# Attention's transposes on VectorE and through DRAM, and the first down product in plain products, in a hybrid decoder layer

## The chip, the cores and the metric

The kernel runs on one core of a Trainium2 chip. The metric is the time of one execution in device microseconds (us). Three runs of the kernel before took 1603.06, 1602.11 and 1602.8 us, so its time is the median, 1602.8 us. One further execution was recorded by the hardware profiler. Its span, from the first to the last instruction, is 1600.6 us.

The engines: TensorE (PE in the profile; its weight loads are PEld) multiplies matrices and accumulates in PSUM; VectorE (DVE), ScalarE (ACT) and GpSimd (POOL) work element by element; SyncE (SP) and GpSimd also issue DMAs.

## The reference

One decoder layer is applied to 256 prompt tokens and to 8 samples of 8 new tokens each, all with the same weights and all in fp32.

```
xn = rms_norm(x, g_mix)
b_gate, c_gate, h_conv, q, k, v, gate_c, gate_a = split(xn @ w_in)     # D = 2048
u = c_gate * h_conv
y_conv = (b_gate * causal_dwconv3(u)) @ w_conv_out
attn = window_attend(q, k, v)          # 16 query heads, 4 kv heads, head 64, window 128
#   s = q k^T / 8 + rel_bias[t5_bucket(dist)];  m = max(s, sink)
#   p = exp(s - m) / (sum exp(s - m) + exp(sink - m));  attn = p v
y_attn = attn @ w_attn_out
h = x + (sigmoid(gate_c) * y_conv + sigmoid(gate_a) * y_attn) @ w_o
hn = rms_norm(h, g_ffn)
h = h + (silu(hn @ w_gate) * (hn @ w_up)) @ w_down                     # FF = 5632
y = rms_norm(h, g_fin)
```

The prompt attends within itself in bands of 128 queries; each sample attends to 128 cached keys and its own 8. Outputs are y, the last 128 rows of k and v, and the convolution's state, for both groups.

## The kernel before, in words

All 320 tokens (256 + 64) are the columns of every tile, and features lie on the 128 partitions. Each weight is read once from memory in tiles of 512 KB (`wraw`, 4 buffers, DMAs issued by SP). ScalarE copies a tile to a reduced format (`whi`, L128) and VectorE subtracts that from it (`wlo`, L129; 3 buffers each). The activations are kept as two parts in the same way. A product is three matmuls for each block of 128 features by 128 outputs, high weight by high rows, high weight by low rows, low weight by high rows, each with 320 columns and the sum in PSUM (`product`, L175 is its matmul). The low one is issued three blocks later (`passes`), which gives VectorE time. A weight tile gives 24 such matmuls. The rows stand in memory in an interleaved pattern of 16 by 5 by 4 (`fives`, `turns`, `row_tiles`), and the products' matmuls read them through it.

TensorE's order is the order of the program: kv, then q, then four rounds of C, H and B (the convolution), then eight rounds of gate_conv, gate_attn and the two output projections (`gc`, `ga`, `yc`, `ya`), then `wo`, then the feed-forward layer in two halves of 28 and 16 blocks of 128 features, each with its gate and up products (`fg`, `fu`) and then its down product, then the last norm. Attention has no stage of its own. It is a generator that `product` advances by a step after each weight tile (`tick`), so its instructions stand between the products' tiles on every engine, in the order in which the code yields: eight units of a kv head and two query heads for the prompt (scores, softmax, normalisation, four 128 by 128 transposes `pp` at L586 which TensorE makes from the weights of attention and `ident`, two masked copies `pT`, then `po`, weights by values), then the samples (scores `pss`, transposes `spp` and `spn`, weights by values `spo`). k and v of the tokens are turned into rows by TensorE too (`pk`, L493 and L496). The relative bias is put in place as one matmul with a one-hot table (`pe_`, L441); it is stored in DRAM (`e_scr`) and read back as a shifted band per unit (`bias`, L523).

The norms' sums over partitions are matmuls by ones (`over_partitions`, L200): `prb` for the first norm, `pss2` for the second, each with two parts that lie contiguously in memory. A `nudge` (L196) is one matmul into a scratch bank that nobody reads; there are four: within kv, ahead of the third q product, ahead of the second `fg`, and ahead of the second half's first `fu`.

The first half's down product (`down(0, c0)`, L962, L966, L970, four times 512 outputs) has, for each 128 features, a moving operand of 512 columns for the high weight (`a_move`, 128 of its columns the low part of tokens), a matmul with the high weight as the moving operand (`dl`, L966, 512 columns), and one of 320 columns for the low weight.

## Time and profile before

| | us |
|---|---|
| three runs | 1603.06, 1602.11, 1602.8 |
| median | 1602.8 |
| profiled execution, span | 1600.6 |
| median of the runs less the span | 2.2 |
| TensorE busy in the span | 1592.1 (99%) |
| VectorE | 885.6 (55%) |
| ScalarE | 651.4 (41%) |
| GpSimd | 78.3 (5%) |

The profile's page gives busy time by engine, the span in 40 slices, the DMA queues, the chain of work that ended last, and groups of instructions by line. The timeline gives single instructions: the start of one, its length and its count if equal ones follow each other. Matmuls overlap, so the length of one (0.30 us) is not its price. The price is the distance from one start to the next.

### The profile page before, as it was taken

To read this page: it belongs to the slowest core of one execution; us is meant where nothing else is said; L and a number is where in the kernel's file an instruction comes from. 1 tells how busy PE (TensorE), PEld (TensorE's weight loads), DVE (VectorE), ACT (ScalarE), POOL (GpSimd) and SP (SyncE) were. 2 spreads that over 40 slices of the span, in tenths; PEclk is the share of its full clock that TensorE was granted. 3 is DMA by queue.
4 is the path that set the end of the run, shared out by engine and by line. 5 is a ranking of instruction groups with operands and counts; after the bars stand their busy time and mean duration, and the time that the engine had idled before them with its cause. 6 is when DMAs were issued, how large, how long until landed. Compare 5 with 4: busy or idle time off the path is not lost.

```text
span 1600.6 us, 26409 instructions
## 1 busy us (share of the span) xinstructions
PE 1592.1 (99%) x10957; PEld 1555.5 (97%) x10957; DVE 885.6 (55%) x1316; ACT 651.4 (41%) x928; POOL 78.3 (5%) x123
## 2 busy tenths in 40 slices
PE   9999999999999999999999999999999999999998
PEld 9999999999999999999999999998888999999887
DVE  7879565444455555556555555553444455555556
ACT  7555433433333334444333333333333334344443
POOL 1101311000000003320000000000000000000000
PEclk9999999999999999999999999999999999999999
DMA  7554546545444545544444445455555544545552
GB/s 276 174 170 137 182 145 200 167 158 156 154 157 157 157 157 159 158 158 155 154 157 156 157 157 159 158 158 158 155 154 155 157 156 158 158 158 157 182 175 93
DMA packets 74400, 258.14 MB, mean 161 GB/s; under 512 B 8552, under 2 KB 11928, under 8 KB 74152
## 3 DMA queue, kind: packets, MB, share of 16 engines
q1 hardware_dynamic: 71880, 249.86, 49.4%
q0 software_dynamic: 1968, 5.90, 1.3%
q8 instruction: 86, 1.41, 0.4%
q10 hardware_dynamic: 432, 0.69, 0.1%
q14 instruction: 34, 0.28, 0.1%
HBM read 253.30 MB, written 5.08 MB: 161 GB/s over the span
## 4 chain that ended last, share of the span: by engine, by line
PE 99%; DVE 0%; ACT 0%; DVEq 0%; issue 0%
PE fu L175 18%; PE fg L175 18%; PE dn L962 9%; PE gc L175 7%; PE ga L175 7%; PE wo L175 7%; PE dn L970 6%; PE B L175 3%; PE C L175 3%; PE H L175 3%; PE q L175 3%; PE yc L175 3%; PE ya L175 3%; PE dl L966 2%; PE kv L366 2%; PE dn L1114 1%
## 5 line engine op out<-in xcount | busy, mean ns | idle before, releaser
L129 DVE TENSOR_TENSOR wlo<-wraw,whi 128x1024 fp32r<-128x1024 f32 (+1 forms) x460 | 561.7, 1221 | 588.7 <-ACT whi L128 580.5
L128 ACT ACTIVATE whi<-wraw 128x1024 fp32r<-128x1024 f32 (+1 forms) x460 | 485.0, 1056 | 717.3 <-PE dn L962 144.7
L962 PE MATMUL dn<-a_t,whi 128*128 128x512 f32 x640 | 211.1, 385 | 0.0
L175 PE MATMUL fu<-hh_t,whi 128*128 128x320 f32 x704 | 205.3, 302 | 0.0
L175 PE MATMUL fg<-hl_t,whi 128*128 128x320 f32 x704 | 205.3, 302 | 0.0
L175 PE MATMUL fu<-hl_t,whi 128*128 128x320 f32 x704 | 205.3, 302 | 0.0
L175 PE MATMUL fg<-hh_t,whi 128*128 128x320 f32 x704 | 205.3, 302 | 0.0
L175 PE MATMUL fg<-hh_t,wlo 128*128 128x320 f32 x704 | 159.0, 302 | 0.0
L175 PE MATMUL fu<-hh_t,wlo 128*128 128x320 f32 x704 | 159.0, 302 | 0.0
L970 PE MATMUL dn<-a_t,wlo 128*128 128x320 f32 x640 | 146.8, 302 | 0.0
L962 PEld LDWEIGHTS dn<-a_t,whi 128*128 128x128 f32 x640 | 118.8, 188 | 19.3
L175 PEld LDWEIGHTS fg<-hh_t,whi 128*128 128x128 f32 x704 | 131.9, 187 | 0.0
L175 PEld LDWEIGHTS fu<-hh_t,whi 128*128 128x128 f32 x704 | 131.9, 187 | 0.0
L175 PEld LDWEIGHTS fg<-hl_t,whi 128*128 128x128 f32 x704 | 131.8, 187 | 0.0
L175 PEld LDWEIGHTS fu<-hl_t,whi 128*128 128x128 f32 x704 | 131.8, 187 | 0.0
L970 PEld LDWEIGHTS dn<-a_t,wlo 128*128 128x128 f32 x640 | 111.2, 188 | 9.3
L175 PEld LDWEIGHTS fu<-hh_t,wlo 128*128 128x128 f32 x704 | 116.3, 187 | 0.0
L175 PEld LDWEIGHTS fg<-hh_t,wlo 128*128 128x128 f32 x704 | 116.3, 187 | 0.0
L175 PE MATMUL ga<-xl_t,whi 128*128 128x320 f32 x256 | 74.6, 301 | 0.0
L175 PE MATMUL gc<-xl_t,whi 128*128 128x320 f32 x256 | 74.6, 302 | 0.0
L175 PE MATMUL wo<-m_l,whi 128*128 128x320 f32 x256 | 74.6, 302 | 0.0
L175 PE MATMUL gc<-xh_t,whi 128*128 128x320 f32 x256 | 74.6, 301 | 0.0
(313 smaller groups left out, 2681.4 us busy)
## 6 DMA issues: line engine op xcount, KB each, us to landing
wraw<-in_w_in_dram SPq DMA_DIRECT2D x128, 512.0 KB, 3.8
wraw<-in_w_gate_dram SPq DMA_DIRECT2D x88, 512.0 KB, 3.8
wraw<-in_w_up_dram SPq DMA_DIRECT2D x88, 512.0 KB, 3.7
wraw<-in_w_down_dram SPq DMA_DIRECT2D x88, 512.0 KB, 3.6
wraw<-in_w_o_dram SPq DMA_DIRECT2D x32, 512.0 KB, 3.7
wraw<-in_w_conv_out_dram SPq DMA_DIRECT2D x16, 512.0 KB, 3.6
wraw<-in_w_attn_out_dram SPq DMA_DIRECT2D x16, 512.0 KB, 3.6
wraw<-in_w_kv_dram SPq DMA_DIRECT2D x6, 512.0 KB, 7.4
```

What stands on the lines that cost most here:

```text
L128: last["hi"] = nc.scalar.activation(hi, src, AF.Copy)
L129: last["lo"] = nc.vector.tensor_sub(lo, src, hi.bitcast(F32))
L175: last["mm"] = nc.tensor.matmul(turns(fives(ps[c][:, :T])), w[:, k, c * P:(c + 1) * P], turns(x(kc)), start=(kc == 0 and i == 0), stop=(kc ...
L366: last["mm"] = nc.tensor.matmul(turns(fives(ps[c][:, :T])), w[:, k, c * P:(c + 1) * P], turns(x(kc)), start=(kc == 0 and m == 0), stop=(kc ...
L962: nc.tensor.matmul(turns(placed(ps[c])), parts[k][0][:, cs], turns(a_move(k)), start=k == 0, stop=False)
L966: nc.tensor.matmul(low, a_low(k), parts[k][0], start=k == 0, stop=k == nf - 1 and c0 < E0)
L970: last["mm"] = nc.tensor.matmul(turns(placed(ps[c])[:, :, 0:JT]), parts[k][1][:, cs], turns(a_move(k)[:, :, 0:JT]), start=False, stop=k == ...
L1114: nc.tensor.matmul(turns(placed(ps[c])[:, :, JR:]), held[k][0][:, cs], turns(a_move(k)[:, :, JR:]), start=k == 0, stop=k == nf - 1,)
```

## The change

Every transpose of attention leaves TensorE. VectorE transposes 32 by 32 blocks within SBUF (`nc.vector.transpose`), GpSimd's DMAs write the result to a DRAM scratch, in four pieces, one for each group of 32 partitions, so that the blocks also change places (`turned_rows`), and one more DMA reads it back. This holds for k and v (`kv_turn`, then a ScalarE copy in `kv_natural`), for the eight units of the prompt (`prompt_turn`, read back and masked in SBUF in `prompt_values`, a new step after all eight units) and for the samples (`s_scr`, `n_scr`). The one-hot matmul becomes 17 copies on GpSimd. The sums of the norms (`prb`, `pss2`) read their parts through the products' pattern, from rows of tiles that are free at that time (`two_rows`). The last two prompt units' `po` come in one group.

Two nudges go (ahead of the second `fg` and of the second half's first `fu`), and three of 320 columns come: behind `pss`, behind `spo` and ahead of the first `ga`. The first half's down product becomes plain products: three matmuls of 320 columns per block, from rows in the products' pattern (`a_fives`); the results go to `hT` alone.

```diff
-    def two_parts(src, tags=("ta", "tb")):
-
-        n = src.shape[-1]
-        hi, lo = (wk.tile([P, UL], F32R, tag=t, name=u("part"))[:, :n] for t in tags)
-        nc.scalar.activation(hi, src, AF.Copy)
-        nc.vector.tensor_sub(lo, src, hi.bitcast(F32))
+    def two_rows(src, hi, lo):
+
+        nc.scalar.activation(hi, fives(src), AF.Copy)
+        nc.vector.tensor_sub(lo, fives(src), hi.bitcast(F32))
         return hi, lo
...
         for i, x in enumerate(parts):
-            nc.tensor.matmul(out, ones_r, x, start=i == 0, stop=i == 1)
+            nc.tensor.matmul(turns(fives(out)), ones_r, turns(x), start=i == 0, stop=i == 1)
...
+    def turned_rows(name, flipped, blocks, run):
+
+        scr = dr.tile([blocks * B, 4 * run], F32, name=name)
+        rows = scr.rearrange("(b i) (a x) -> a i b x", i=B, x=run)
+        for a_ in range(4):
+            nc.gpsimd.dma_start(rows[a_], flipped[a_ * B:(a_ + 1) * B].rearrange("p (b x) -> p b x", x=run))
+        return scr
...
-    rel = zz.tile([NBK, NH], F32, name="rel")
+    relT = zz.tile([NH, NBK], F32, name="relT")
...
-        parts = two_parts(xacc)
-        nc.vector.tensor_copy(oh_r, oh)
-        nc.scalar.activation(rel_r[:, 0], rel, AF.Copy)
-        nc.vector.tensor_sub(rel_r[:, 1], rel, rel_r[:, 0].bitcast(F32))
-        yield
-        prb, pe_ = ps_aux("prb"), ps_aux("pe_")
-        for i in range(2):
-            nc.tensor.matmul(pe_[:NH, :WIN], rel_r[:, i], oh_r, start=i == 0, stop=i == 1)
+        parts = two_rows(xacc, at_h(7), at_l(7))
+        at, one_each = [_bucket(c) for c in range(WIN)], NBK // 2
+        nc.gpsimd.tensor_copy(e_sb[:, WIN - 1:WIN - 1 + one_each], relT[:, :one_each])
+        for b in range(one_each, NBK):
+            c, n = WIN - 1 + at.index(b), at.count(b)
+            nc.gpsimd.tensor_copy(e_sb[:, c:c + n], relT[:, b:b + 1].to_broadcast([NH, n]))
+        yield
+        prb = ps_aux("prb")
         over_partitions(prb[:, :T], parts)
...
-        nc.vector.tensor_copy(e_sb[:, WIN - 1:2 * WIN - 1], pe_[:NH, :WIN])
         nc.gpsimd.dma_start(e_scr, e_sb)
...
-    def kv_natural(t):
+    def kv_turn(t):
+
         t0, tn = TOK[t]
-        pk = ps_aux(u("pk"))
-        for j in range(2):
-            nc.tensor.transpose(pk[:tn, j * P:(j + 1) * P], vT[:, j, t0:t0 + tn], ident)
-        if t > 0:
-            for j in range(2):
-                nc.tensor.transpose(pk[:tn, 256 + j * P:256 + (j + 1) * P], kT[:, j, t0:t0 + tn], ident)
-        nc.vector.tensor_copy(vn[t][:tn, :], pk[:tn, 0:DKV])
+        nb, zs = tn // B, (vT, kT)[:1 + (t > 0)]
+        run = len(zs) * 2 * B
+        flipped = pr.tile([P, 512], F32, tag="T", name=u("kvT"), bufs=3)[:, :nb * run]
+        blocks = flipped.rearrange("p (b z c j) -> p z c b j", b=nb, c=2, j=B)
+        for i, z in enumerate(zs):
+            nc.vector.transpose(blocks[:, i], z[:, :, t0:t0 + tn].rearrange("p c (b i) -> p c b i", i=B))
+        rows = pr.tile([P, 512], F32, tag="rows", name=u("rows"), bufs=3)[:tn, :4 * run]
+        nc.gpsimd.dma_start(rows, turned_rows(f"kv_scr{t}", flipped, nb, run))
+        return rows.rearrange("p (a z c j) -> p z a c j", a=4, c=2, j=B)
+
+    def kv_natural(t, rows):
+        t0, tn = TOK[t]
+
+        def natural(out, z):
...
+        natural(vn[t], 0)
         if t > 0:
-            nc.vector.tensor_copy(kn[:tn, :], pk[:tn, 256:512])
...
-    def prompt_pt(s):
-        pt = pr.tile([P, 3, 2 * WIN], F32, tag="pT", name=u("pT"), bufs=4)
-        pp = ps_aux(u("pp"))
-        for n in range(4):
-            nc.tensor.transpose(pp[:, n * WIN:(n + 1) * WIN], s[:, n], ident)
-        nc.scalar.activation(pt[:, 0, :], pp[:, 0:256], AF.Copy)
-        for b in range(2):
-            nc.vector.tensor_mul(
-                pt[:, 1 + b, :].rearrange("p (g q) -> p g q", g=2),
-                pp[:, 256:512].rearrange("p (g q) -> p g q", g=2),
-                sides[:, b:b + 1].to_broadcast([P, 2, WIN]),
-            )
-        return pt
+    def prompt_turn(s):
+        flipped = pr.tile([P, 4, 4, B], F32, tag="T", name=u("T"), bufs=3)
+        nc.vector.transpose(flipped.rearrange("p b n j -> p n b j"), s.rearrange("p n (b i) -> p n b i", i=B))
+        return turned_rows(u("p_scr"), flipped.rearrange("p b n j -> p (b n j)"), 4, 4 * B)
+
+    def by_head(x):
+
+        return x.rearrange("p a g j -> p g a j")
+
+    def prompt_masked(pv, sides, pt):
+
+        late = by_head(pt[:, :, 2:4])
+        side = pv.tile([P, 2, 4, B], F32, name=u("side"))
+        for out, m in ((side, 0), (late, 1)):
+            mask = sides[:, m].rearrange("p (a j) -> p a j", j=B).unsqueeze(1).to_broadcast([P, 2, 4, B])
+            nc.vector.tensor_mul(out, late, mask)
+        return by_head(pt[:, :, 0:2]), side, late
...
                 nc.tensor.matmul(
-                    po[par * 64:(par + 1) * 64, b * 256:(b + 1) * 256],
-                    vn[t][:, kv * HD:(kv + 1) * HD], pts[par][:, kb, :], start=st_, stop=sp_,
+                    po[par * 64:(par + 1) * 64, b * 256:(b + 1) * 256].rearrange("p (g a j) -> p g a j", g=2, j=B),
+                    vn[t][:, kv * HD:(kv + 1) * HD], pts[par][kb], start=st_, stop=sp_,
...
+    def prompt_weights(scrs):
+        bias, sc, sm = {}, {}, {}
         bias[0] = bias_load(*units[0])
-        for i in range(len(units) + 3):
...
                 yield
                 sm[i] = prompt_softmax(*units[i], sc[i])
-            if i >= 3 and (i - 3) % 4 == 3:
-                for n in (i - 5, i - 3):
-                    kv, gp = units[n]
-                    prompt_pv(kv // 2, gp, (pts.pop(n - 1), pts.pop(n)))
-            if 0 <= i - 2 < len(units):
-            if 0 <= i - 1 < len(units):
+            if i >= 1:
                 prompt_norm(sc[i - 1], *sm.pop(i - 1))
-            if i >= len(units):
-                yield
+                scrs.append(prompt_turn(sc.pop(i - 1)))
+
+    def prompt_values(pv, scrs):
+        sides = pv.tile([P, 2, WIN], F32, name="sides")
...
+        pts = []
+        for i in range(len(units) + 5):
+            if i < len(units):
+                pts.append(pv.tile([P, 4, 4, B], F32, name=u("pT")))
+                nc.gpsimd.dma_start(pts[i].rearrange("p a n j -> p (a n j)"), scrs[i])
+            if i >= 5:
+                pts[i - 5] = prompt_masked(pv, sides, pts[i - 5])
+            yield
+        for i in range(0, len(units), 2):
+            kv, gp = units[i]
+            prompt_pv(kv // 2, gp, pts[i:i + 2])
+        yield
...
     def sample_attention(sm):
-        kf = sm.tile([P, NB, 2, W2], F32, name="kf")
+        kf = sm.tile([P, NB, 2, W2], F32, tag="kf", name="kf")
...
+        nudge(xh, xl, T)
...
-        pn = sm.tile([P, NB, TS], F32, name="pnew")
-        nc.vector.tensor_copy(pn, s[:, :, WIN:W2])
-        yield
-        ptw = sm.tile([P, NB * P], F32, name="ptw")
-        for h in range(2):
+        flipped = sm.tile([P, NB * W2], F32, tag="kf", name="sT")
+        nc.vector.transpose(
+            flipped[:, :NB * WIN].rearrange("p (c b j) -> p b c j", c=4, j=B),
+            s[:, :, 0:WIN].rearrange("p b (c i) -> p b c i", i=B),
+        )
+        nc.vector.transpose(flipped[:, NB * WIN:], s[:, :, WIN:W2])
+        ptw = sm.tile([P, NKV, NB, B], F32, name="ptw")
+        nc.gpsimd.dma_start(
+            ptw.rearrange("p a b j -> p (a b j)"), turned_rows("s_scr", flipped[:, :NB * WIN], 4, NB * B)
+        )
         pns = sm.tile([64, P], F32, name="pns")
-        nc.vector.tensor_copy(pns, pp[:64, 0:P])
+        nc.gpsimd.dma_start(pns, turned_rows("n_scr", flipped[:, NB * WIN:], 2, B))
+        yield
+        yield
+        yield
+        yield
...
                     nc.tensor.matmul(
                         pos[j][par * 64:(par + 1) * 64, b * 32:(b + 1) * 32],
-                        cv[:, kv * HD:(kv + 1) * HD], ptw[:, b * P + kv * 32:b * P + (kv + 1) * 32],
+                        cv[:, kv * HD:(kv + 1) * HD], ptw[:, kv, b],
...
+        nudge(xh, xl, T)
...
+        rows = []
         for t in range(3):
-            kv_natural(t)
+            rows.append(kv_turn(t))
             yield
         yield from keys_twice()
+        for t in range(3):
+            kv_natural(t, rows[t])
+            yield
...
     def attention():
-        yield from prompt_attention()
+        scrs = []
+        yield from prompt_weights(scrs)
         pr_p.close()
+        with tc.tile_pool(name="pv", bufs=1, side="right") as pv:
+            yield from prompt_values(pv, scrs)
         with tc.tile_pool(name="sm", bufs=1, side="right") as sm:
...
+            if (mp, nm) == (0, "ga"):
+                nudge(xh, xl, T)
...
+    def a_fives():
+
+        per = FH[0] // 2
+        step = per * JS + 16
+        group = -(-(NS * step - 16) // JS) * JS
+        flat = fp.tile([P, LEAD_F + A_ALL], F32R, tag="at", name=u("a_t"))
+        groups = [rows_in(flat, LEAD_C + g * group, step, lambda k: k % per * JS) for g in range(4)]
+        return [lambda k, i=i: groups[2 * i + k // per](k) for i in range(2)]
...
+    def sets_of(nf):
+        sets = [(k, k + 1) for k in range(0, nf, 2)]
+        sets[-2:] = [sets[-2] + sets[-1]]
+        return sets
+    def down_first(c0):
+
+        nf = FH[0]
         ps = [ps_acc(u("dn")) for _ in range(4)]
+        sets = sets_of(nf)
+        for i, ks in enumerate(sets):
             parts = {}
+            for k in ks[::2]:
+                parts |= down_weights(0, c0, k)
             end = i == len(sets) - 1
-            order = [(k, c) for k in parts for c in range(4)]
+            order = [(k, c) for k in ks for c in range(4)]
+            if end or i == 0:
+                order.sort(key=lambda kc: kc[1])
+            for k, c, m in passes(order, end):
+                w, x = ((0, a_hi), (0, a_lo), (1, a_hi))[m]
+                last["mm"] = nc.tensor.matmul(
+                    turns(fives(ps[c][:, :T])), parts[k][w][:, c * P:(c + 1) * P], turns(x(k)),
+                    start=k == 0 and m == 0, stop=k == nf - 1 and m == 2,
+                )
+        for c in range(4):
+            k = c0 // P + c
+            nc.vector.tensor_add(hT[:, k, :], ps[c][:, :T], hT[:, k, :])
...
-        a_move, a_low, a_first, free = a_rows(half)
+        if half == 0:
+            a_hi, a_lo = a_fives()
+        else:
+            a_move, a_low, a_first, free = a_rows(half)
...
-            if half == 0 and fpair == 1:
-                nudge(hh, hl, P)
...
-                over_partitions(pss[:, :T], two_parts(hacc, ("tc", "td")))
+                over_partitions(pss[:, :T], two_rows(hacc, a_hi(FH[0] - 1), a_lo(FH[0] - 1)))
...
-            if half == 1 and fpair == 0:
-                nudge(hh, hl, P)
...
+                if half == 0:
+                    split_to(a_hi(f), a_lo(f), fives(gs[c]))
+                    continue
...
-                if half == 1:
-                    nc.scalar.activation(a_first(f), gs[c][:, 0:P], AF.Copy)
+                nc.scalar.activation(a_first(f), gs[c][:, 0:P], AF.Copy)
...
         for c0 in range(0, D if half == 0 else E0, 512):
-            down(half, c0)
-            if half == 1:
+            if half == 0:
+                down_first(c0)
+            else:
+                down(c0)
```

How the order of instructions changes is shown at three places.

TensorE in the first H product beside attention: `pp` are the four transposes of one prompt unit, the rows around it the product's own matmuls. Before:

```order
L175 MATMUL H_1318<-xh_t,wlo_1375 128x16x5x4
L175 MATMUL H_1319<-xh_t,wlo_1375 128x16x5x4
L586 MATMUL pp_1414<-ident,s_1172 128x128 x4
L175 MATMUL H_1318<-xh_t,whi_1424 128x16x5x4
L175 MATMUL H_1318<-xl_t,whi_1424 128x16x5x4
```

After:

```order
L176 MATMUL H_1334<-xh_t,wlo_1398 128x16x5x4
L176 MATMUL H_1335<-xh_t,wlo_1398 128x16x5x4
L176 MATMUL H_1334<-xh_t,wlo_1398 128x16x5x4
L176 MATMUL H_1335<-xh_t,wlo_1398 128x16x5x4
L176 MATMUL H_1334<-xh_t,whi_1438 128x16x5x4
L176 MATMUL H_1334<-xl_t,whi_1438 128x16x5x4
```

The transposes are gone and one tile's matmuls follow the other's directly.

VectorE in the same stretch, where `den` is a unit's denominator, `s` its weights, `pT` the masked copy of a former unit's transposes and `wlo` a weight tile's low part. Before:

```order
L129 TENSOR_TENSOR wlo_1555<-wraw_1552,whi_1554 128x1024
L577 TENSOR_TENSOR den_1403<-den_1403,es_1404 128x4
L578 RECIPROCAL den_1403<-den_1403 128x4
L589 TENSOR_TENSOR pT_1413<-pp_1414,sides 128x256 x2
L580 TENSOR_SCALAR s_1358<-s_1358,den_1403 128x128 x4
L129 TENSOR_TENSOR wlo_1607<-wraw_1604,whi_1606 128x1024
```

After:

```order
L130 TENSOR_TENSOR wlo_1567<-wraw_1564,whi_1566 128x1024
L582 TENSOR_TENSOR den_1426<-den_1426,es_1427 128x4
L583 RECIPROCAL den_1426<-den_1426 128x4
L585 TENSOR_SCALAR s_1381<-s_1381,den_1426 128x128 x4
L589 STREAM_TRANSPOSE T_1600<-s_1381 128x4x4x32
L130 TENSOR_TENSOR wlo_1626<-wraw_1623,whi_1625 128x1024
```

The two masked copies have left this place, and one transpose of 128 by 512 stands behind the unit's own normalisation, ahead of the next weight tile's low part.

TensorE in the first half's down product, where `a_t` holds the activations and `dn` the four sums. Before:

```order
L962 MATMUL dn_11267<-a_t_7524,whi_11322 128x16x8x4
L966 MATMUL dl_11271<-whi_11322,a_t_7524 128x512
L962 MATMUL dn_11268<-a_t_7524,whi_11322 128x16x8x4
L962 MATMUL dn_11269<-a_t_7524,whi_11322 128x16x8x4
L962 MATMUL dn_11270<-a_t_7524,whi_11322 128x16x8x4
L970 MATMUL dn_11267<-a_t_7524,wlo_11323 128x10x8x4
```

After:

```order
L1015 MATMUL dn_11259<-a_t_7576,whi_11355 128x16x5x4 x2
L1015 MATMUL dn_11260<-a_t_7576,whi_11355 128x16x5x4 x2
L1015 MATMUL dn_11261<-a_t_7576,whi_11355 128x16x5x4 x2
L1015 MATMUL dn_11262<-a_t_7576,whi_11355 128x16x5x4 x2
L1015 MATMUL dn_11259<-a_t_7576,wlo_11356 128x16x5x4
```

Nine matmuls of 512, 512 and 320 columns per block become twelve of 320, in the pattern (16x5x4) that the other products have.

## Rows read from the trace of the kernel before

**Rows 1.** The page: busy time by engine; TensorE's granted clock in 40 slices.

```profile
PE 1592.1 (99%) x10957; PEld 1555.5 (97%) x10957; DVE 885.6 (55%) x1316; ACT 651.4 (41%) x928; POOL 78.3 (5%) x123
...
PEclk9999999999999999999999999999999999999999
```

**Rows 2.** The page: the chain of work that ended last, by engine.

```profile
PE 99%; DVE 0%; ACT 0%; DVEq 0%; issue 0%
```

**Rows 3.** TensorE's timeline, wo and the next product: start us, us, operation, xcount.

```profile
593.92 0.30 PE L175 MATMUL wo<-m_h,whi 128*128 128x320 f32 x1
...
701.45 0.30 PE L175 MATMUL fg<-hh_t,whi 128*128 128x320 f32 x1
```

**Rows 4.** TensorE's timeline at a prompt unit's transposes.

```profile
110.29 0.60 PE L586 MATMUL pp<-ident,s 128*128 128x128 f32 x4
110.64 0.39 PE L175 MATMUL H<-xh_t,whi 128*128 128x320 f32 x1
110.87 0.30 PE L175 MATMUL H<-xl_t,whi 128*128 128x320 f32 x1
```

**Rows 5.** TensorE's timeline at the samples' transposes.

```profile
210.04 1.04 PE L700 MATMUL spp<-ident,s_s 128*128 128x128 f32 x8
...
210.94 0.39 PE L175 MATMUL H<-xh_t,whi 128*128 128x320 f32 x1
211.17 0.30 PE L175 MATMUL H<-xl_t,whi 128*128 128x320 f32 x1
```

**Rows 6.** TensorE's timeline at the one-hot product and the first norm's sum.

```profile
38.50 0.58 PE L175 MATMUL q<-xh_t,wlo 128*128 128x320 f32 x3
39.01 0.29 PE L441 MATMUL pe__589<-oh_r,rel_r 32*16 32x128 f32 x2
...
39.62 0.30 PE L175 MATMUL q<-xh_t,whi 128*128 128x320 f32 x1
```

**Rows 7.** TensorE's timeline from the second norm's sum over a nudge.

```profile
715.18 0.31 PE L175 MATMUL fu<-hh_t,whi 128*128 128x320 f32 x1
...
728.85 0.23 PE L196 MATMUL nudge<-hh_t,hl_t 128*128 128x128 f32 x1
...
729.11 0.30 PE L175 MATMUL fg<-hl_t,whi 128*128 128x320 f32 x1
...
742.40 0.30 PE L175 MATMUL fu<-hh_t,whi 128*128 128x320 f32 x1
```

**Rows 8.** TensorE's timeline, first down product and the product behind it.

```profile
1078.40 0.38 PE L962 MATMUL dn<-a_t,whi 128*128 128x512 f32 x1
...
1266.96 0.30 PE L175 MATMUL fg<-hh_t,whi 128*128 128x320 f32 x1
...
1280.61 0.23 PE L196 MATMUL nudge<-hh_t,hl_t 128*128 128x128 f32 x1
```

**Rows 9.** Busy time by stretch: us, then PE, PEld, DVE, ACT, POOL, PEclk, DMA share, GB/s.

```profile
88.00:145.00 57.00, 57.00 (x421) 55.70 (x420) 51.82 (x132) 32.57 (x91) 7.93 (x18) 1.00 0.52 162
145.00:185.00 40.00, 40.00 (x293) 38.70 (x292) 26.65 (x58) 17.88 (x36) 13.16 (x24) 1.00 0.54 170
```

**Rows 10.** VectorE's groups, 88 to 180 us: operation xcount | busy, mean ns | idle before.

```profile
L589 DVE TENSOR_TENSOR pT<-pp,sides 128x256 f32<-128x256 f32 x16 | 6.1, 416 | 0.0
...
L562 DVE TENSOR_REDUCE mx<-s 128x4 f32<-128x512 f32 x8 | 5.5, 682 | 0.1
```

**Rows 11.** VectorE's timeline, the first norm's reciprocal.

```profile
41.82 2.15 DVE L234 RECIPROCAL r<-r 128x320 f32<-128x320 f32 x1 [0.54 <-ACT r L233]
```

**Rows 12.** GpSimd's timeline, DMA issues.

```profile
42.49 1.48 POOL L523 DMA_DIRECT2D bias<-e_scr  x2
...
126.18 0.74 POOL L523 DMA_DIRECT2D bias<-e_scr  x1
```

**Rows 13.** DMA issues: transfer, queue, xcount, KB each, us from issue to landing.

```profile
bias<-e_scr POOLq DMA_DIRECT2D x8, 256.0 KB, 4.1
kf<-in_cache_kt_dram POOLq DMA_DIRECT2D x4, 256.0 KB, 5.2
...
e_scr<-e_sb POOLq DMA_DIRECT2D x1, 24.0 KB, 1.8
```

More of the change, by code (lines that the diff above doesn't have):

```diff
@@ L23 @@
 NBK = 32
+B = 32
 FF = 5632
@@ L613, in two_to @@
         nc.vector.tensor_sub(dl, src, dh.bitcast(F32))
-    def prompt_attention():
-        units = [(j * 2 + par, gp) for j in range(2) for gp in range(2) for par in range(2)]
-        bias, sc, sm, pts = {}, {}, {}, {}
+    units = [(j * 2 + par, gp) for j in range(2) for gp in range(2) for par in range(2)]
+    def prompt_weights(scrs):
+        bias, sc, sm = {}, {}, {}
         bias[0] = bias_load(*units[0])
-        for i in range(len(units) + 3):
+        for i in range(len(units) + 1):
             if i < len(units):
@@ L936, in h_parts, with down_weights @@
         return parts_of(hT[:, k, :])
-    def down(half, c0):
-        nf, f0 = FH[half], half * FH[0]
+    def down_weights(half, c0, k0):
+        raw = wp.tile([P, 2, 512], F32, tag="wraw", name=u("wraw"), bufs=4)
+        k = half * FH[0] + k0
+        nc.sync.dma_start(raw, w_d[c0 // 512, :, k:k + 2, :])
+        hi = wp.tile([P, 2, 512], F32R, tag="whi", name=u("whi"), bufs=3)
+        lo = wp.tile([P, 2, 512], F32R, tag="wlo", name=u("wlo"), bufs=3)
+        split_to(hi, lo, raw)
+        return {k0 + j: (hi[:, j, :], lo[:, j, :]) for j in range(2)}
@@ L957, in down @@
+    def down(c0):
+        nf = FH[1]
+        ps = [ps_acc(u("dn")) for _ in range(4)]
+        low = ps_aux(u("dl"))
+        sets = sets_of(nf)
+        for i, ks in enumerate(sets):
+            parts = {}
+            for k in ks[::2]:
+                parts |= down_weights(1, c0, k)
+            end = i == len(sets) - 1
+            order = [(k, c) for k in ks for c in range(4)]
             if end or i == 0:
@@ L966, in down @@
                     nc.tensor.matmul(
-                        low, a_low(k), parts[k][0], start=k == 0, stop=k == nf - 1 and c0 < E0
+                        low, a_low(k), parts[k][0], start=k == 0, stop=k == nf - 1
                     )
@@ L983, in down @@
             mark["out"].append(nc.vector.tensor_add(rest, rest, got[:, :, JT:]))
[L984 to L989 removed]
+        nc.scalar.activation(ylow[:, c0:c0 + 512], low, AF.Copy)
     for half in range(2):
@@ L1153, in hybrid_layer @@
         for m, x in enumerate((xhk, xlk)):
-            last["mm"] = nc.tensor.matmul(rowacc, x, wh, start=False, stop=k == nf - 1 and m == 1)
+            last["mm"] = nc.tensor.matmul(rowacc, x, wh, start=k == m == 0, stop=k == nf - 1 and m == 1)
         if k == 3:
@@ L1213 @@
     from concourse.bass_utils import run_bass_kernel_spmd as _run
-    onehot = _np.zeros((NBK, WIN), _np.float32)
-    for c in range(WIN):
-        onehot[_bucket(c), c] = 1.0
     block = _np.zeros((64, NB), _np.float32)
@@ L1248 @@
     arrays, args, outs = {}, {}, []
-    for name, v in [(n, inputs[n]) for n in _INS] + [("c_onehot", onehot), ("c_block", block)]:
+    for name, v in [(n, inputs[n]) for n in _INS] + [("c_block", block)]:
         v = _np.ascontiguousarray(v)
```

52 lines of the change are left out of this document (12 added, 40 removed).

## The prediction, made before the changed kernel ran

> **What bounds the kernel now.** I read the page first: TensorE is busy for 99% of the span, and its granted clock stands at nine tenths or more in all 40 slices [rows 1], which is its upper level of 2.4 GHz. The chain of work that ended last is TensorE for 99% of it [rows 2]. So the time is the sum of TensorE's instruction stream, and an edit is worth what it adds to or takes from that stream, unless it makes TensorE wait.
>
> Then I read the stream's pace from the timeline, as distances between starts. wo has 8 x 16 x 6 = 768 matmuls from 593.92 to 701.45 [rows 3]: 107.53 / 768 = 0.1400 us each. This is the good pace. There is a second one. Behind the sum `pss2`, fu's 96 matmuls take from 715.18 to 728.85, 0.1424 each; from the first matmul behind the nudge, at 729.11, the 95 up to 742.40 go at 0.1399 again [rows 7]. Behind the first down product the same: 1266.96 to 1280.61 is 0.1422 each, up to another nudge [rows 8]. So an odd matmul can leave the stream in a pace 2.3 ns slower per matmul, which lasts until another disturbance; a nudge ended it both times.
>
> **The change part by part, on TensorE.**
>
> Prompt transposes: four `pp` take from 110.29 to 110.64, and the product's next matmul takes 0.23 up to 110.87 where the pace is 0.14 [rows 4]. One unit costs 0.35 + 0.09 = 0.44 us. Eight units: -3.5.
>
> k and v: ten transposes of the same width, in groups of 2, 4 and 4. By [rows 4], 0.44 for each group of four and half of 0.35 for the pair: -1.1.
>
> Samples: nine transposes from 210.04 to 210.94, and 0.23 instead of 0.14 behind them [rows 5]: 0.90 + 0.09, so -1.0.
>
> One-hot product and first sum: three matmuls that start at 38.50 should end their turn at 38.92; the next product's starts at 39.62 [rows 6]. The detour costs 0.70. What remains is the sum's two matmuls; if they run at the good pace, 0.28: -0.4.
>
> The second sum now reads rows in the products' pattern, which should leave no slow pace behind: 96 x 2.4 ns = -0.23 in fu. Behind the down product likewise 96 x 2.2 ns = -0.21 in fg.
>
> Two nudges go. One costs 729.11 - 728.85 = 0.26 where a matmul costs 0.14, so 0.12 each: -0.24 [rows 7]. Three of 320 columns come, at a matmul's 0.14 each: +0.42. One of `po`'s two groups goes, which I put at one such switch, -0.1.
>
> First down product: 112 block rows of nine matmuls take from 1078.40 to 1266.96, 188.56 us [rows 8]. Columns per block row are 4 x 512 + 512 + 4 x 320 = 3840 before and 12 x 320 = 3840 after. 112 x 12 = 1344 matmuls at 0.1400 give 188.16: -0.4. The reorder loses nothing, because the old form already streamed at its columns. If the new rows ran at the slow pace, 1344 x 2.3 ns = +3.1; they have the products' pattern and lie with the products' offsets, so I take the good one.
>
> Sum: -3.5 - 1.1 - 1.0 - 0.4 - 0.23 - 0.21 - 0.24 + 0.42 - 0.1 - 0.4 = -6.8 us.
>
> **What lies beside TensorE, and what it costs if the cover is gone.**
>
> VectorE gains eight transposes of 128 x 512 at the scores, and loses there sixteen masked copies of 0.416, 6.7 us, which return later out of SBUF [rows 10]. No row of before has this transpose. From below, it can't cost less than nothing. From above, the slowest row is the reciprocal, 2.15 us for 320 elements per partition [rows 11], 3.4 for 512. I take the row of its shape, the reduction of 128 x 512, 0.682 [rows 10]: 8 x 0.68 = 5.5, so VectorE's load there stays what it was, 51.82 of 57 us between 88 and 145 [rows 9]. Its cover is the low parts made ahead: three buffers of 24 matmuls, 3.36 us each, so VectorE may run about 6 us late before TensorE waits. The masks return between 145 and 185, where it is busy for only 26.65 of 40. At 3.4 us per transpose, VectorE would need 51.8 - 6.7 + 27.2 = 72.3 us in those 57, and TensorE would wait for some 72.3 - 57 - 6 = 9 us.
>
> The Trainium skill speaks against this edit: "VectorE: DVE Perf Modes", Rules for kernel authors, leaves a 128 x 128 transpose to TensorE where the result may go to PSUM, and its section on the three transpose paths gives 390 ns for TensorE, and 311 ns for VectorE, for 32 x 32 blocks only. The trace has TensorE at about 0.11 us each within the stream, and no row for VectorE. By the page's figure an estimate for one unit is 4 x 0.311 = 1.24 us, 9.9 in all, which would fill 55 of the 57 us and cost little or nothing.
>
> ScalarE loses the prompt's copies out of PSUM and is busy for 32.57 of 57 us [rows 9], so its part is nothing.
>
> The round trips are cover against queue. By the order of the changed program GpSimd issues 98 DMAs where it had 34. An issue takes 0.74 us, also at 126.18 in the stretch where VectorE is at 91% [rows 9, 12], and transfers land 1.8 to 5.2 us after the issue [rows 13]. A unit's trip is four issues, a landing, one issue and a landing: 4 x 0.74 + 1.8 + 0.74 + 2, about 7.5 us. For the prompt, a unit's rows are read back at least four tiles, 13.4 us, ahead of their mask. For the samples, the transposes, eight issues and two landings in a row come to about 12 us against the four added yields, 13.4 us. The samples' cached keys (`kf`), loaded only after `po`, need four issues and 5.2, about 8.2, against about 13.4. So each is hidden, the samples' one with the least to spare. Behind a waiting DMA on GpSimd's queue stand the bias loads of later units and the convolution's products with rb; those are wanted at the end of B, a product of 96 matmuls or 13.4 us later. TensorE's order puts no product behind the round trips but `po` and `spo`, and a wait there holds up everything.
>
> **Rivals.**
>
> A: the forecast, all hidden. 1600.6 - 6.8 = 1593.8 span. The median of the runs lies 2.2 us above the profiled span, so 1596.0. Own range 1594.5 to 1597.5: the terms of the small groups and that 2.2 are each good to about half a microsecond.
>
> B: VectorE becomes the bound between 88 and 145. For it: 91% busy already. Against it: the masks leave. From a transpose of about 1.5 us (51.8 - 6.7 + 12 = 57.1) its lead begins to be eaten, and at 3.4 the wait is 9 us. 1596 to 1605; middle 1599.
>
> C: a round trip is late. For it: 64 more DMAs in order on one queue, trips whose cover exceeds them by only 1 to 6 us. Against it: no issue in the trace is held up by VectorE. Twice the landing times on the samples' trip and on `kf` would give waits of 3 to 6 us: 1599 to 1602.
>
> D, the other side: the slow pace sticks where a nudge has gone or does not take. From the first ga to the last fu of the second half there are 8544 matmuls of 320 columns with no nudge among them (2208 in the rounds of gates, 768 in wo, 22 pairs of 192 in the halves, 1344 in the first down product); at 2.3 ns each the whole is 19.6 us: 1596.0 + 19.6 = 1615.6. It decides from 6.8 / 0.0023 = 2960 matmuls, that is if the slow pace lasts for over some 415 us. For it: two nudges are removed exactly where the slow pace stood before, and both places now rest on the pattern alone. Against it: what left it behind was a sum over contiguous parts and matmuls of 512 columns, and neither is there any more; each change between products of the pattern keeps 0.140 [rows 3].
>
> E: the change saves nothing because the transposes lay in gaps that TensorE has anyway. Against it: there is no gap in the stream around them, and the product's matmuls start 0.14 apart up to the transposes [rows 4, 6]. The time would be 1602.8.
>
> **How the numbers follow.** A 0.70, B 0.10, C 0.10, D 0.07, E 0.03. This kernel's runs can tell about 0.2%, 3.2 us, from no change, so faster means below 1599.6 and slower above 1606.0. Faster: all of A, over half of B, a quarter of C and a little of D, 0.80. Slower: D and the far end of B, 0.08. The same: the rest, 0.12. The range 1594.0 to 1601.5 holds A, most of C and half of B or more; D is left out above.
>
> **What would show it.** In the profile after: no `pp`, `pk` or `spp` on TensorE, and its busy share still at 99%. A product's distance between starts of 0.140 in the first fu, in the second half's first fg and all through the first down product, which takes 188.2 us. STREAM_TRANSPOSE of 128 x 512 near 0.7 us, and VectorE near 91% while scores run. TensorE's waits ahead of `po` and `spo` at nothing. Wrong would be a distance of 0.142 over many products (D), waits of TensorE for `wlo` between 88 and 145 (B), or for `ptw`, `pns` or `pT` (C).

## The result, and the profile after

The changed kernel takes 1607.5 us (median of six runs, 1607.36 to 1607.69) against 1602.8: a ratio of 1.0031 with an interval of 1.0019 to 1.0042. The forecast was 1596.0, faster. It is slower.

The page after, busy time by engine and the chain that ended last by engine:

```profile
PE 1597.2 (99%) x11241; PEld 1581.5 (98%) x11241; DVE 884.7 (55%) x1258; ACT 646.9 (40%) x894; POOL 118.1 (7%) x204
...
PE 99%; DMA 1%; ACT 0%; DVE 0%; ACTq 0%; DVEq 0%; issue 0%
```

TensorE still ends the chain with 99%, as in [rows 1, 2]. So again only its stream has to be read. TensorE's timeline after, at the places of [rows 3, 7, 8] (start us, us, operation, xcount):

```profile
588.25 0.30 PE L176 MATMUL wo<-m_h,whi 128*128 128x320 f32 x1
...
695.77 0.30 PE L176 MATMUL fg<-hh_t,whi 128*128 128x320 f32 x1
...
709.22 0.45 PE L199 MATMUL pss<-a_t,ones_r 128*128 128x320 f32 x2
709.50 0.30 PE L176 MATMUL fu<-hh_t,whi 128*128 128x320 f32 x1
...
723.15 0.30 PE L176 MATMUL fg<-hh_t,whi 128*128 128x320 f32 x1
...
1078.14 0.45 PE L1015 MATMUL dn<-a_t,whi 128*128 128x320 f32 x2
...
1269.29 0.30 PE L176 MATMUL fg<-hh_t,whi 128*128 128x320 f32 x1
...
1487.74 0.39 PE L1040 MATMUL dn<-a_t,whi 128*128 128x512 f32 x1
```

Three stretches tell it all. Up to wo, the changed kernel is 593.92 - 588.25 = 5.7 us ahead, and wo itself runs at 0.140. Behind `pss2`, 96 matmuls of fu take 709.50 to 723.15, 0.1422 each; the down product's 1344 take 191.15 us, 0.1422 each, where before the whole product took 188.56; and the pace holds up to 1487.74, where the second half's down product begins. From fu to there it is 778.24 us. The kernel before had 767.15, from 715.18 [rows 7] to this row of its timeline:

```profile
1482.33 0.38 PE L962 MATMUL dn<-a_t,whi 128*128 128x512 f32 x1
```

So 11.1 us are lost, and 5.7 - 11.1 = -5.4 is the difference of the spans, 1606.0 against 1600.6. From that down product to the end both take 118.3.

What was to be hidden is hidden. Busy time by stretch after (us, PE, PEld, DVE, ACT, POOL, PEclk, DMA share, GB/s), against [rows 9]:

```profile
88.00:145.00 57.00, 57.00 (x417) 57.00 (x416) 53.12 (x132) 31.30 (x86) 21.33 (x42) 1.00 0.62 187
145.00:185.00 40.00, 40.00 (x288) 40.00 (x287) 32.46 (x58) 16.28 (x25) 15.79 (x31) 1.00 0.73 238
```

and VectorE's groups after, 88 to 180 us:

```profile
L130 DVE TENSOR_TENSOR wlo<-wraw,whi 128x1024 fp32r<-128x1024 f32 x26 | 31.9, 1232 | 3.6 <-ACT whi L129 3.3
...
L589 DVE STREAM_TRANSPOSE T<-s 128x512 f32<-128x512 f32 x8 | 5.7, 708 | 0.1
...
L602 DVE TENSOR_TENSOR side<-pT,sides 128x256 f32<-128x256 f32 x6 | 3.8, 625 | 0.8 <-issue 0.8
```

A transpose of 128 x 512 takes 0.708 us where 0.68 was put. VectorE is 93% busy at the scores, and TensorE fills both stretches.

### The profile page after: what moved, and what is told of

The parts are those of the page before. It is cut to its first block, busy times and chain, and to the rows that moved or that the text cites. A ratio compares the mean times of both kernels' runs of the same rounds, so it can differ in the third digit from the quotient of the medians.

```text
span 1606.0 us, 26991 instructions
## 1 busy us (share of the span) xinstructions
PE 1597.2 (99%) x11241; PEld 1581.5 (98%) x11241; DVE 884.7 (55%) x1258; ACT 646.9 (40%) x894; POOL 118.1 (7%) x204
## 4 chain that ended last, share of the span: by engine, by line
PE 99%; DMA 1%; ACT 0%; DVE 0%; ACTq 0%; DVEq 0%; issue 0%
PE fu L176 19%; PE fg L176 19%; PE dn L1015 12%; PE ga L176 7%; PE wo L176 7%; PE gc L176 7%; PE B L176 3%; PE q L176 3%; PE H L176 3%; PE C L176 3%; PE ya L176 3%; PE yc L176 3%; PE dn L1040 3%; PE dn L1048 2%; PE kv L370 1%; PE dl L1044 1%
## 5 line engine op out<-in xcount | busy, mean ns | idle before, releaser
L1015 PE MATMUL dn<-a_t,whi 128*128 128x320 f32 x896 | 165.0, 303 | 0.0
L1015 PEld LDWEIGHTS dn<-a_t,whi 128*128 128x128 f32 x896 | 139.2, 187 | 0.0
L1015 PE MATMUL dn<-a_t,wlo 128*128 128x320 f32 x448 | 105.4, 304 | 0.0
L1015 PEld LDWEIGHTS dn<-a_t,wlo 128*128 128x128 f32 x448 | 75.2, 187 | 0.0
L176 PE MATMUL ga<-xh_t,whi 128*128 128x320 f32 x256 | 74.6, 301 | 0.0
```

The costliest lines, as they stand in the source:

```text
L176: last["mm"] = nc.tensor.matmul(turns(fives(ps[c][:, :T])), w[:, k, c * P:(c + 1) * P], turns(x(kc)), start=(kc == 0 and i == 0), stop=(kc ...
L1015: last["mm"] = nc.tensor.matmul(turns(fives(ps[c][:, :T])), parts[k][w][:, c * P:(c + 1) * P], turns(x(k)), start=k == 0 and m == 0, stop= ...
```

## The experiments

The question is why `pss2` left the slow pace, though its rows were read in the products' pattern, and whether that is the whole loss. The good pace is 0.140 us per matmul, the slow one 0.142. The theories: **N**, the slow pace lasts until some other matmul ends it, and the removed nudge was what ended it; **O**, the sum leaves it because its weights, `ones_r`, lie at another place than a product's weights. In the program as built `ones_r` starts 160 bytes past a multiple of 256, every weight tile 128 past one, and every product's rows, those of `pss2` among them, 64 past one. The rivals: **P**, the plain down product is slow by itself; **R**, the pattern is what leaves the slow pace; **Q**, rows and weights must both be like a product's.

**One nudge back** (e1_nudge_back).

```diff
+            if half == 0 and fpair == 1:
+                nudge(hh, hl, P)
             psg = product(
```

> The changed kernel with one nudge put back, ahead of the second fg product, where the kernel before had it; nothing else differs. Theory N (the loss is the slow pace that the second norm's sum leaves behind, which nothing ends any more until the second half's down product): the 96 matmuls of the first fu stay at 0.142 us each, all 5376 matmuls behind the nudge run at 0.140, which takes 5376 x 2.2 ns = 11.8 us off the 1607.5, less 0.15 for the nudge: 1595.8 us. Rival P (the slow pace belongs to the new places of the activations in the plain down product, and would come with or without the nudge): the down product's 1344 matmuls stay at 0.142, the nudge helps only the pairs ahead of it: about 1601 us.

1595.59 us; ratio to before 0.9954 (0.9939 to 0.9969). TensorE's timeline:

```profile
709.32 0.30 PE L176 MATMUL fu<-hh_t,whi 128*128 128x320 f32 x1
...
722.97 0.22 PE L195 MATMUL nudge<-hh_t,hl_t 128*128 128x128 f32 x1
...
723.23 0.30 PE L176 MATMUL fg<-hl_t,whi 128*128 128x320 f32 x1
...
736.53 0.30 PE L176 MATMUL fu<-hh_t,whi 128*128 128x320 f32 x1
```

fu still takes 13.65 us for 96 (0.1422); behind the nudge 95 take 13.30 (0.140). One instruction gives back 11.9 us of 1607.5. N holds, and P falls: the plain down product runs at 0.140 if it is entered at 0.140.

**The kernel before without its nudge** (e4_before_no_nudge).

```diff
-            if half == 0 and fpair == 1:
-                nudge(hh, hl, P)
```

> The kernel before with one line less: the nudge ahead of the second fg is gone, all else as it was. Theory N (the slow pace that the second norm's sum leaves lasts until something else than a product's matmul comes, and the nudge was all that ended it): the 26 products of pairs two to fourteen, 2496 matmuls, run at 0.1423 instead of 0.1400, +5.7 us, less the nudge's 0.1; the first down product's matmuls of 512 columns then end it: 1608.3 us. Rival (the slow pace would fade by itself, at a product's end or a load): within 1 us of the kernel before, 1602 to 1604 us.

1608.37 us; ratio 1.0033 (1.0020 to 1.0047). The pace does not fade: the last fu ahead of the down product still takes 13.66 for 96.

```profile
1070.71 0.30 PE L175 MATMUL fu<-hh_t,whi 128*128 128x320 f32 x1
...
1084.37 0.38 PE L962 MATMUL dn<-a_t,whi 128*128 128x512 f32 x1
```

So in the kernel before too, one nudge was worth 5.4 us (the kernel before took 1603.01 in these runs). The old down product takes 188.61 us behind the slow pace, 188.56 before, so the loss ended there; the plain one carries it on.

**The ones moved** (e2_ones_moved), no nudge added.

```diff
-    ones_r = cst.tile([P, P], F32R, name="ones_r")
+    ones_r = cst.tile([P, P + 64], F32R, name="ones_r")[:, 56:56 + P]
```

> The changed kernel without any further nudge; only the ones that serve as weights in the norms' sums lie elsewhere, 128 bytes past a multiple of 256, as all weight tiles do, where they lay 160 bytes past one. Theory O (the sum's matmuls leave the slow pace because their weights start at another place within 256 bytes than the products' weights): the two pss2 matmuls take 0.140 each and the first fu behind them 0.140, no slow pace anywhere in the feed-forward layer: 1595.5 us. Theory N in its plain form (any pair that isn't a product's leaves the slow pace, whatever its operands' places): 1607.5 us, unchanged.

1595.53 us; ratio 0.9955 (0.9938 to 0.9971).

```profile
708.93 0.44 PE L199 MATMUL pss<-a_t,ones_r 128*128 128x320 f32 x2
709.21 0.30 PE L176 MATMUL fu<-hh_t,whi 128*128 128x320 f32 x1
...
722.65 0.30 PE L176 MATMUL fg<-hh_t,whi 128*128 128x320 f32 x1
...
1072.09 0.44 PE L1015 MATMUL dn<-a_t,whi 128*128 128x320 f32 x2
...
1260.24 0.30 PE L176 MATMUL fg<-hh_t,whi 128*128 128x320 f32 x1
```

The sum's pair takes 0.28, fu 13.44 (0.140), the down product 188.15. At this place O holds: with the weights 224 bytes further on, the sum takes what two more matmuls of a product would take, and the pace behind it stays. Every later tile moves by 256 bytes with it, but that is not the cause: the probes below have the same shift with the ones at 160, and there `pss2` leaves fu at 0.142.

**The sum from contiguous parts** (e3_sum_contiguous), and **with the ones moved as well** (e5_contiguous_ones_moved).

```diff
-                over_partitions(pss[:, :T], two_rows(hacc, a_hi(FH[0] - 1), a_lo(FH[0] - 1)))
+                over_contiguous(pss[:, :T], two_parts(hacc, ("tc", "td")))
```

> The changed kernel, with the second norm's sum alone read from contiguous parts again, as before; no nudge behind it. Theory R (reading the parts through the products' pattern is what leaves the slow pace): the pace behind it would be 0.140 and the time 1595.6 us. Theories N and O (the sum leaves it in either form, as it did in the kernel before, where fu behind the contiguous sum ran at 0.1424): unchanged within 0.5 us, 1607.5 us.

> The changed kernel without a further nudge, the second sum read from contiguous parts (as in the kernel before) and the ones moved to 128 bytes past a multiple of 256. Theory O alone (only the weights' place decides): fu behind the sum runs at 0.140, 1595.6 us. Rival Q (the pair must be like a product's matmul in both operands, rows in the pattern and weights at 128, to leave the pace alone): the contiguous pair takes over 0.14 each, the slow pace stands behind it, 1607.5 us.

e3 takes 1607.72 us, ratio 1.0031 (1.0019 to 1.0042); e5 1607.48, ratio 1.0028 (1.0017 to 1.0038). e5's timeline:

```profile
708.96 0.45 PE L211 MATMUL pss<-part,ones_r 128*128 128x320 f32 x2
709.25 0.31 PE L176 MATMUL fu<-hh_t,whi 128*128 128x320 f32 x1
...
722.92 0.30 PE L176 MATMUL fg<-hh_t,whi 128*128 128x320 f32 x1
```

fu takes 13.67. R falls, and O alone falls too. At this place Q holds: the changed reading of the rows was needed, and so was the ones' place. As a rule for any pair it is not shown. In the probes below, five contiguous pairs, with ones at 64, 128 or 160, all left 0.140. Those read rows that start 64 bytes past a multiple of 256, as a product's do; in e5 the second of the two parts starts at 96, and no run separates that from the pattern.

**Probes** (p1_probes, p2_probes_320): extra groups ahead of fg, in p1 with nudges of 128 columns ahead of fu, in p2 of 320.

```diff
+    def odd(phase, n=2, flat=False, cols=T):
+        w = ones_w[:, (phase - 160) % 256 // 4:][:, :P]
...
+            if (half, fpair) in probes:
+                odd(*probes[half, fpair])
+            elif (half, fpair) != (0, 0):
+                nudge(hh, hl, T)
```

> The changed kernel with extra matmuls into a bank that nobody reads, each ahead of an fg product, and a nudge ahead of each fu, so that each extra group starts from the good pace and its effect is read from the 96 matmuls behind it. The extra groups: pairs that read rows through the products' pattern with ones as weights at 0, 32, 64, 96, 128, 160, 192 and 224 bytes past a multiple of 256; one matmul of 160 and one of 128; three and four of 160; pairs and single ones from contiguous columns. Theory O: the pairs at 128 leave 0.140, most others, 160 among them, leave 0.142. Theory N in its plain form: every pair leaves 0.142 behind, whatever its place. A third reading (the pace is a phase which each extra matmul shifts by a bit, so that the count decides): one, two, three and four matmuls at 160 differ from each other. Time about 1598 us, as the nudges cost some 0.2 us each where they change nothing.

> The probes again, with nudges of 320 columns between them instead of 128, since the nudges of 128 columns turned the good pace into the slow one in 10 of the 14 places where they met it in the earlier probes. Extra pairs ahead of fg: ones at 0, 32, 64, 96, 128, 160, 192, 224; one at 160 and at 128, three and four at 160; contiguous pairs, four and single ones; narrow contiguous ones. If a nudge of 320 columns sets the good pace whatever it meets (the five in the attention of the changed kernel were each followed by 0.140), every fu runs at 0.140, and each fg shows what its pair does to the good pace: theory O expects 0.140 behind 128 bytes and 0.142 behind 160. If instead each extra matmul only shifts a phase, some fu run at 0.142, and no form is a reset. Time 1599 to 1606 us accordingly.

p1 (one run, 1610.45 us) did not give what it was made for: its narrow nudges are no reset. They turned the slow pace into the good one in all 8 places, and the good one into the slow one in 12 of 15 (the expectation of p2 says 10 of 14, a miscount). The first two in a row left fg good, between 723 and 737, and fu behind it slow:

```profile
723.05 0.22 PE L195 MATMUL nudge<-hh_t,hl_t 128*128 128x128 f32 x1
...
736.61 0.22 PE L195 MATMUL nudge<-hh_t,hl_t 128*128 128x128 f32 x1
...
736.87 0.31 PE L176 MATMUL fu<-hl_t,whi 128*128 128x320 f32 x1
...
750.38 0.31 PE L1074 MATMUL odd<-hh_t,ones_r 128*128 128x320 f32 x1
```

From 736.87 to 750.38, 95 matmuls take 13.51, 0.1422 each. In p2 (one run, 1605.62 us, with 23 wide nudges and 19 groups to pay for) all 23 nudges of 320 columns left 0.140 behind, four of them out of the slow pace. So each group starts from the good one. Pairs through the pattern left 0.140 with ones at 0, 32, 64, 96, 128 and 224 bytes, and 0.142 at 160 and 192. Only those at 0 and 128 took 0.140 each themselves; the others took 141.5 to 144.5 ns on the mean. The pairs at 128 and at 160:

```profile
859.75 0.30 PE L1074 MATMUL odd<-hh_t,ones_r 128*128 128x320 f32 x1
...
860.03 0.30 PE L176 MATMUL fg<-hh_t,whi 128*128 128x320 f32 x1
...
873.47 0.31 PE L195 MATMUL nudge<-hh_t,hl_t 128*128 128x320 f32 x1
...
887.08 0.30 PE L1074 MATMUL odd<-hh_t,ones_r 128*128 128x320 f32 x1
...
887.37 0.30 PE L176 MATMUL fg<-hh_t,whi 128*128 128x320 f32 x1
...
901.02 0.31 PE L195 MATMUL nudge<-hh_t,hl_t 128*128 128x320 f32 x1
```

860.03 to 873.47 is 13.44, 887.37 to 901.02 is 13.65. One, three and four matmuls at 160 left 0.140, two left 0.142. So beside the place the count matters, as the third reading of p1 has it; what each matmul would shift is not shown. Nor does the place decide by itself: the pair at 192 met the good pace in both probes and left 0.140 in p1, 0.142 in p2. Pairs at 0 and 128 changed nothing, in p1 too, where they met the slow pace and left it standing. O said that most unlike places leave 0.142; in p2 two of six do.

The first norm's sum, `prb`, shows more of it. It has the same weights and the same pattern as `pss2`, and in the changed kernel it did the opposite: q came to it in the slow pace and went on in the good one.

```profile
33.31 0.30 PE L176 MATMUL q<-xl_t,whi 128*128 128x320 f32 x1
...
39.71 0.45 PE L199 MATMUL prb<-at_t,ones_r 128*128 128x320 f32 x2
39.99 0.30 PE L176 MATMUL q<-xh_t,whi 128*128 128x320 f32 x1
...
60.15 0.31 PE L195 MATMUL nudge<-xh_t,xl_t 128*128 128x320 f32 x1
```

Ahead of it 45 matmuls take 6.40, 0.1422 each; behind it 144 take 20.16, 0.1400. In e3 and p1 it did the same, and in e1 and p2, where q came at 0.140, it left 0.142. So a pair at 160 that reads through the pattern does not lead to the slow pace as such: it turned the pace that it met into the other in all 11 places where the traces of the changed kernel, e1, e3, p1 and p2 have one (three times slow to good, eight times good to slow). With the ones at 128, `prb` left whichever pace it met: the good one in e2, e7 and e9, the slow one in e5 and e8. Where q's slow pace came from is not shown.

**A narrow nudge in the good pace** (e9_ones_moved_narrow_nudge): e2 with e1's nudge.

```diff
+            if half == 0 and fpair == 1:
+                nudge(hh, hl, P)
```

> The changed kernel with the ones moved, and one nudge of 128 columns ahead of the second fg, in the good pace: the very instruction that made the changed kernel faster by 12 us when it met the slow pace. If such a nudge flips the pace (in the first probes it turned the good one into the slow one in 12 of 15 places and the slow one into the good one in all 8), the 5376 matmuls behind it run at 0.142: 1595.5 + 11.9 = 1607.4 us. If a nudge only ever ends a slow pace, or the good pace that is left by plain products is not disturbed by it: 1595.7 us.

1607.31 us; ratio 1.0028 (1.0017 to 1.0040).

```profile
722.00 0.22 PE L195 MATMUL nudge<-hh_t,hl_t 128*128 128x128 f32 x1
...
722.25 0.31 PE L176 MATMUL fg<-hl_t,whi 128*128 128x320 f32 x1
...
735.77 0.30 PE L176 MATMUL fu<-hh_t,whi 128*128 128x320 f32 x1
```

95 matmuls in 13.52, 0.1423 each. The instruction that gains 11.9 us in e1 costs 11.8 here. Either of two right edits alone is worth 12 us; both together are worth nothing.

**The plain down product alone** (e6_plain_down_alone): the kernel before with the feed-forward part of the changed one, the old sum and the nudge ahead of the second fg.

```diff
-            down(half, c0)
-            if half == 1:
+            if half == 0:
+                down_first(c0)
+            else:
+                down(c0)
...
-            if half == 1 and fpair == 0:
-                nudge(hh, hl, P)
```

> One part of the change alone: the kernel before with the first half's down product in plain products (and without the nudge in the second half's first pair), while the attention, the norms' sums and the nudge ahead of the second fg are as before. By the prediction's terms: the down product takes 1344 x 0.140 = 188.2 us instead of 188.56, fg behind it 0.2 less, a nudge 0.1 less: 1602.1 us. Rival P (the plain form itself runs at 0.142 in these rows): 1605.0 us or more, with the second half's pairs slow behind it, up to 1609 us.

1602.25 us; ratio 0.9995 (0.9985 to 1.0004), no change that can be told. In its trace the product takes what the prediction put, 1267.38 - 1079.21 = 188.17, and fg behind it 13.43:

```profile
1079.21 0.30 PE L977 MATMUL dn<-a_t,whi 128*128 128x320 f32 x1
...
1267.38 0.30 PE L175 MATMUL fg<-hh_t,whi 128*128 128x320 f32 x1
...
1280.81 0.30 PE L175 MATMUL fu<-hh_t,whi 128*128 128x320 f32 x1
```

**Less cover for the samples' round trip** (e8_three_yields_less): e2 with three of the four added steps taken out.

```diff
         yield
-        yield
-        yield
-        yield
         ptn = sm.tile([64, NB, P], F32, name="ptn")
```

> The changed kernel with the ones moved, and with three of the four added steps between the samples' transposes and their use taken out, so that TensorE comes to spo three weight tiles, 10.1 us, earlier. It tests the prediction's term for the samples' round trip through DRAM (about 12 us against 13.4 of cover). In the run with the ones moved, pns had landed and ptn was made by 246.8 us, 5.1 us ahead of spo at 251.9. If the trip takes the same time here, TensorE waits 10.1 - 5.1 = 5 us, ahead of spo or for a low weight part that stands behind ptn on VectorE: 1600.5 us. If the trip was stretched only because nothing waited for it, or VectorE's lead hides the rest: 1595 to 1597 us.

1598.77 us, ratio 0.9980 (0.9968 to 0.9992), between the two answers put, and the six executions differ: three at 1596.9 to 1597.2, three at 1600.3 to 1602.9, the latter with a mean granted clock of 0.995 to 0.997 where the others have 0.999. The profiled one is of the first kind:

```profile
246.89 0.43 PE L742 MATMUL spo<-ptn,vn 64*64 64x256 f32 x2 [1.35 <-DVE ptn L732]
```

`spo` came to its turn at 246.89 - 1.35 = 245.54, two tiles ahead of e2's 251.86 and not three, so the 5.1 us of margin left it 1.2 short: a wait of 1.35. The trip through DRAM ends at the same time, `ptn` starting at 245.62 against 245.54; with the four steps TensorE is covered by 5 us. The span is 1.7 longer than e2's, and the rest of that is q, which ran at 0.142 up to its nudge here (144 x 2.2 ns = 0.3). None of the three longer executions was profiled, so why they differ stays open.

**Fewer nudges** (e7_fewer_nudges): e2 without the nudges ahead of the third q product, behind `spo` and ahead of the first ga.

```diff
-            if (j, gp) == (1, 0):
-                nudge(xh, xl, T)
...
-        nudge(xh, xl, T)
...
-            if (mp, nm) == (0, "ga"):
-                nudge(xh, xl, T)
```

> The changed kernel with the ones moved (128 bytes past a multiple of 256), and with three nudges less: ahead of the third q product, behind spo and ahead of the first ga. In the run with the ones moved each of these stood between products that ran at 0.140 on either side, and cost about 0.15 us. Theory O: the pace stays at 0.140 in q, behind spo and in ga, and the time is 1595.5 - 0.45 = 1595.1 us. Rival (one of the three still ends a slow pace that comes in some executions, or that the other two leave): a stretch of 0.142 from that place on; if it is the last, up to the first down product of the second half, 9000 matmuls x 2.2 ns: 1615 us.

1594.71 us; ratio 0.9948 (0.9936 to 0.9960): the fastest of all, 0.5% below the kernel before. Its gain over e2 is 0.8 us between medians, and the intervals overlap. In the trace q's 336 matmuls behind the first sum run at 0.140 to the end:

```profile
39.65 0.30 PE L176 MATMUL q<-xh_t,whi 128*128 128x320 f32 x1
...
86.69 0.30 PE L176 MATMUL C<-xh_t,whi 128*128 128x320 f32 x1
```

That does not show the nudge ahead of the third q product to be useless. In the traces of e5 and e8, with the ones moved as well, q came to the first sum in the slow pace and kept it, 144 matmuls in 20.48 us, until this nudge ended it. The trace here is of an execution in which q came at 0.140; over q's 336 matmuls the slow pace would cost 0.7 us, and the five executions lie between 1594.49 and 1594.81.

## Why the prediction was wrong

**The step that failed** is "The second sum now reads rows in the products' pattern, which should leave no slow pace behind: 96 x 2.4 ns = -0.23 in fu". It took one difference between the sum and a product, the rows, for all of it. The weights differ too, by where they lie, and that decided: in the changed kernel the rows alone did not keep the good pace, in e5 the weights alone did not, in e2 both did. With that term two others fell: "Two nudges go", -0.24, took away what ended the pace, and "I take the good one" for the down product, whose 1344 matmuls inherited the slow one. In numbers: 5472 matmuls from the first fu to the last, 2.22 ns each, +12.1. The forecast's sum and this give 1593.8 + 12.1 = 1605.9 for the span; 1606.0 was measured.

**The rival** that came true is D, which had 0.07. Its mechanism and its price per matmul are right. Its place is not: it was counted from the first ga, 8544 matmuls and 1615.6, and it begins at `pss2`. [rows 7] stood there for this: a slow pace behind the sum, a nudge, the good pace behind. The count of matmuls up to the next disturbance, which the change raises from 96 to 5472 at that place, gives its price, 12.1; what spoke against it was an argument from likeness, not a row.

**What was right.** The terms up to wo: predicted -5.7 (the transposes, the one-hot product, the three nudges, `po`), measured -5.7, and that match is in part luck. The first 16 us, ahead of the nudge in kv, took 0.6 longer than before (15.82 against 15.26), and they vary in the traces from 15.09 to 15.85, with the old attention too (15.81 in e6). From that nudge to wo it is 572.43 against 578.67, so the terms themselves gave -6.2. The down product: 188.16 put, 188.15 and 188.17 measured in e2 and e6. The span without the slow pace: 1593.8 put, 1593.5 (e2) and 1594.0 (e1). B did not come: 0.708 us per transpose against 0.68, VectorE at 53.1 of 57 us, no wait of TensorE. The estimate by the Trainium skill ("VectorE: DVE Perf Modes", The three transpose paths) was 1.24 us for four blocks of 128 columns, from a figure for bf16; the trace has 0.708 in fp32, so the measurement decides. The page's rule, which leaves such a transpose to TensorE, would have kept a cost here, where TensorE is the bound. C did not come either, with a margin of 5.1 us at the samples, but not for the reason given. The trip that was put at 12 took 14.3 in e2's trace, from the transposes' start at 231.27 to `ptn`'s start at 245.54, and VectorE did wait for it, 1.89 us ahead of `ptn`. The four yields, 13.4, did not cover it; TensorE did not wait because the code has two more steps between `ptn` and `spo`, which the prediction did not count. An issue of these transfers took 0.55 us instead of 0.74, but the transfers landed later than put, 4.0 us in the median for `p_scr` and 5.1 for its reading back, against 1.8 and 2.

## What to carry to other kernels

Where one engine's stream is the time, look at its pace and not only at its waits: here 1.6% of pace over 5472 equal matmuls cost 12.1 us and outweighed all the edits of single ones, and a rare instruction in between set it. Before an instruction that looks useless is removed, measure the stretch that starts behind it, and count how many instructions would inherit what it prevents. If a foreign instruction must stand in a stream, make it like its neighbours in every operand, here rows in their pattern and weights at their place within 256 bytes, rather than repair behind it.

## What the runs showed of the hardware

- Matmuls of 128 x 128 by 320 columns ran at one of two steady paces, 140.0 and 142.2 ns, at the same granted clock (a mean of 0.998 to 0.999 in every profiled execution). In the feed-forward layer either lasted as long as only products of 320 columns followed: 5472 matmuls in the changed kernel.
- What changed it, in both directions: pairs through the pattern with weights at 160 bytes past a multiple of 256 (11 of 11 places), and nudges of 128 columns (20 of 23 in p1). What led out of the good one in some places and not in others: a pair at 192 (p2, not p1), and contiguous pairs (as the second sum in e3 and e5, in none of the three places of the probes that met it). What left either as it was: pairs through the pattern with weights at 0 or 128. What led to the good one: 320 contiguous columns in one nudge, in 23 of 23 places in p2, four of them out of the slow pace. What in the chip makes the two paces was not shown; no run tells a collision of reads from anything else.
- VectorE's transposes of 32 x 32 blocks took 0.708 us for 128 x 512 and 1.234 for 128 x 1024 in fp32.
